# Two heads' v projections in one, and a mixed result written in place, in a hybrid decoder trunk

## The chip, the cores and the metric

The kernel runs on one core of a Trainium2 chip. The metric is the device time of one execution in microseconds (us). A core has TensorE (matrix products, into the accumulator memory PSUM), VectorE, ScalarE and GpSimd (element-wise work), and queues that issue transfers between the chip's main memory (DRAM here) and its on-chip memory (SBUF). The profile calls these engines PE (its weight loads PEld), DVE, ACT, POOL and SP.

## What is computed

Two layers over a residual stream of 1024 positions and 2048 channels, all in float32. Only layer 0 is touched by the change. Its mixer, cut to what matters:

```python
proj = h @ w_in                                   # 2048 -> 7 x 1024
a_u, a_v, a_z, q, k, v, b_z = split(proj)         # each 8 heads of 128 columns
# gating heads, in chunks of 128 positions
vh = rms_norm(gelu(a_v))                          # over each head
s = einsum('hts,bnshd->bnthd', tril(w_s), vh) + b_s
out_a = gelu(a_u) * s * silu(a_z)
# attention heads: stick-breaking, strictly causal, in blocks of 128 queries
z = q @ k.T / sqrt(128)
w = exp(log_sigmoid(z) + later)                   # later: sums of log_sigmoid(-z) to the right
out_b = (w @ v) * silu(b_z)
y = concat(out_a, out_b) @ w_out
```

Ahead of it, a modulation (silu(c) @ w_mod) gives shift, scale and gate of each layer. Layer 1 is a state-space layer whose matrices are prepared from small parameters.

## The kernel before

**Products.** Float32 weights are split exactly into two parts (`split`, L180 on ScalarE and L181 on VectorE), and each product is three matmuls (`mm3`, L205 to L208). `gemm` (L210) loads weights in raw chunks of 128 x 1024 elements, splits them in pieces of 512, and keeps four accumulators, one in each of the four PSUM banks of `ps_mm`; k is the outer loop, so all four banks are in use from the first to the last piece. At the end the banks are emptied one by one by `evac`; the next `gemm` gets its banks in turn. The buffers of a piece (`whi`, `wlo`) and of a raw chunk are three each.

**Layer 0, head by head.** The loop at L623 goes over eight pairs of a gating head and an attention head. In the order of the program, head h has: for even h above 0, the attention's gate projection of two heads (`bz`, L283 evacuates it); `proj_v` (L490), the gating's and the attention's v of one head; `gate_a(h-1)` (L595), the silu and gelu of the gates of the head before and its output product `sgu_out`, then the gelu of this head's `av`; `sgu_scale` and `sgu_mix` (the norm, then the mixing product `sg_ps` at L528, whose result is written to the tile `sg` at L529); the projection `qk`; `attention(h)`, whose first matmul is `z` (L552) and whose last is `oT` (L580); for heads 0 to 2 the modulation chunks (4, 6, 6 of them; `mod_chunk`, L466), for heads 3 to 7 steps of the state-space preparation (3, 4, 4, 4, 1; `s5_prep`); and the projection `uz`. For heads 2 and 4 `proj_v` stands ahead of `bz`. The table-switching functions of ScalarE are kept in runs (silu, gelu, exp and log) by `TableOrder`.

In `proj_v` the transposed input is the stationary operand (128 positions) and the weights are the moving one: 256 columns, 128 of the gating's v and 128 of the attention's. Positions are done in two halves of four banks. The other projections move 512 columns.

**What sets the order.** The program's order gives priorities. A planner puts the instructions of each engine in a fixed order by these priorities and its own costs, when the kernel is built, and inserts the waits. Tiles are taken from pools: a tag has so many buffers, given out in program order, and a new tile waits for the last reader of the old one. What matters here: `av` has one buffer and `v` two (each for one head); `sg` one; `q`, `k`, `u`, `zg` and the two `bz` one each; `ps_t`, a PSUM pool used by the attention, the column sums of the modulation chunks, the preparation and the mixing weight's transpose, has one; `ps_z` has two.

A modulation chunk streams 16 tiles `mraw` of 128 x 512 through four buffers, adds them up in `macc` on VectorE (L174) and sums over partitions on TensorE into `ps_t` (L158).

Of the kernel before, what the change touches and what calls it, by code (L numbers as in the profile page):

```python
# [18 lines left out]
L = 1024  # L19
# [6 lines left out]
class TableOrder:  # L26
    """Keeps the ScalarE functions that need different tables in separate runs."""
# [36 lines left out]
def hybrid_trunk(ctx: ExitStack, tc: tile.TileContext, x, c, ln_pre_g, ln_post_g, w_mod, b_mod,  # L64
# [75 lines left out]
    def rstd_from(ss, n, cnt, pool, name):  # L140
        """1/sqrt(ss/cnt + eps) of a [128, n] tile: exp(-log/2), then one Newton step."""
        r = pool.tile([128, n], F32, tag=name, name=name)
        v = pool.tile([128, n], F32, tag=name + "v", name=name + "v")
        t = pool.tile([128, n], F32, tag=name + "t", name=name + "t")
        V.tensor_scalar(out=v, in0=ss, scalar1=1.0 / cnt, scalar2=EPS, op0=ALU.mult, op1=ALU.add)
        tab.act(r, v, AF.Ln)
        tab.act(r, r, AF.Exp, scale=-0.5)
        V.tensor_tensor(out=t, in0=r, in1=r, op=ALU.mult)
        V.tensor_tensor(out=t, in0=t, in1=v, op=ALU.mult)
        V.tensor_scalar(out=t, in0=t, scalar1=-0.5, scalar2=1.5, op0=ALU.mult, op1=ALU.add)  # L150
        V.tensor_tensor(out=r, in0=r, in1=t, op=ALU.mult)
        return r

    def col_sums(ps, acc, n):
        """[128, n*128] partial sums -> [128, n] PSUM columns."""
        for i in range(n):
          with hi_prio():
            T.matmul(ps[:, i:i + 1], acc[:, i * 128:(i + 1) * 128], ones, start=True, stop=True)  # L158
# [24 lines left out]
    def load_raw(parts, ncols, dma=dma):  # L183
        """parts: (k, first column, DRAM slice [128, k, n]) -> raw tile [128, RAW]."""
        raw = wp.tile([128, RAW], F32, tag="wraw", name="wraw")
        rv = raw.rearrange("p (k n) -> p k n", n=ncols)
        for k, c0, src in parts:
            dma(out=rv[:, k:k + src.shape[1], c0:c0 + src.shape[2]], in_=src)
        return raw
# [3 lines left out]
    def load_w(parts, ncols, eng=V, raw=None, dma_=dma):  # L193
        """Yields the weight chunk in parts of SUB elements, split."""
        if raw is None:
            with hi_prio():
                raw = load_raw(parts, ncols, dma_)
        for i in range(RAW // SUB):
            with hi_prio():
                h = wp.tile([128, SUB], F32R, tag="whi", name="whi")  # L200
                lo = wp.tile([128, SUB], F32R, tag="wlo", name="wlo")
                split(h, lo, raw[:, i * SUB:(i + 1) * SUB], eng)
            yield h.rearrange("p (k n) -> p k n", n=ncols), lo.rearrange("p (k n) -> p k n", n=ncols)
# [6 lines left out]
    def gemm(nk, ncols, src, banks, evac, name, pre=None, eng=V):  # L210
        """src(k0, k1): parts of the weight rows; banks: (width, f), f(k, w_hi, w_lo) -> operands.

        k outermost, so that every weight chunk is used once; in the last chunk bank by bank."""
        ps = [mm_tile(name) for _ in banks]
        kr, ks = RAW // ncols, SUB // ncols
        k0 = 0
        for ci in range(nk // kr):
            if pre is not None:
                pre(ci)
            for wh, wl in load_w(src(ci * kr, (ci + 1) * kr), ncols, eng):  # L220
                if k0 + ks < nk:
                    for kk in range(ks):
                        for b, (wd, f) in enumerate(banks):
                            mm3(ps[b][:, :wd], *f(k0 + kk, wh[:, kk], wl[:, kk]), k0 + kk == 0, False)
                else:
                    for b, (wd, f) in enumerate(banks):
                        for kk in range(ks):
                            mm3(ps[b][:, :wd], *f(k0 + kk, wh[:, kk], wl[:, kk]), k0 + kk == 0, kk == ks - 1)
                        with hi_prio():
                            evac(b, ps[b])  # L230
                k0 += ks

# [19 lines left out]
    def banks_N(hf):  # L252
        res = []
        for t in range(4):
# [3 lines left out]
            res.append((256, f))  # L258
        return res

# [1 line left out]
    # h^T starts without the shift: its part of the first projections is a bias, and the shift is added to h^T later.  # L262
# [159 lines left out]
    with pool("pa") as pa, pool("pu") as pu_, pool("pst") as pst, pool("pat", 2) as pat, ExitStack() as pm_stack:  # L422
# [15 lines left out]
        def bias_first():  # L438
            """The shift's part of the first projections."""
            for gi, (s0, s1) in enumerate(first):  # L440
                ac = pm.tile([128, 512], F32, tag="macc", name="bacc")[:, 0:256]
                for ci in range(4):
                    if ci < 2:
                        ms = [pm.tile([128, 512], F32, tag="mraw", name="mraw", bufs=4) for _ in range(2)]
                    elif ci == 2:
                        ms = [pa.tile([128, L], F32, tag="sg", name="bw")]
# [19 lines left out]
        def mod_chunk(layer, n0):  # L466
            """512 columns of silu(c) @ w_mod, as partial sums over partitions."""
# [22 lines left out]
        def proj_v(h):  # L490
            av = pa.tile([128, 8, 128], F32, tag="av", name="av")
            v = pa.tile([128, 8, 128], F32, tag="v", name="v", bufs=2)
            st["av"], st["v"] = av, v
            for hf in range(2):
                def evac(b, ps, hf=hf):
                    S.activation(av[:, hf * 4 + b, :], ps[:, 0:128], AF.Copy)
                    st["v_done"] = S.activation(v[:, hf * 4 + b, :], ps[:, 128:256], AF.Copy).ins
                gemm(KT, 256, src_ab(1, 5, h), banks_N(hf), evac, f"v{h}e")

        def sgu_scale(h):  # L500
            """Per-token norm of gelu(v) over the head, in the exp/log run."""
            av = st["av"]
# [7 lines left out]
        def sgu_mix(h):  # L510
            av = st["av"]
# [11 lines left out]
            s = pa.tile([128, L], F32, tag="sg", name="sg")  # L523
# [16 lines left out]
        def attention(h):  # L540
            q, kT, v, bz = st["q"], st["k"], st["v"], st["bz"][h % 2]
# [53 lines left out]
        def gate_a(h):  # L595
            """Gates of gating head h, with gelu of the next head's v."""
# [12 lines left out]
            if h < 7:  # L609
                tab.act(st["av"], st["av"], AF.Gelu_apprx_tanh)  # L610
# [12 lines left out]
        for h in range(8):  # L623
            if h in (2, 4):
                proj_v(h)
            if h > 0 and h % 2 == 0:
                new_bz()
                proj_T(h, 6, None, evac_bz, "bz")
            if h not in (2, 4):
                proj_v(h)  # L630
            gate_a(h - 1)
# [38 lines left out]
    def pairs(ap, k0, cols):  # L670
        """Rows KORD[k0], KORD[k0 + 1] of ap [128, k, n], in one part if adjacent."""
# [314 lines left out]
def s5_prep(nc, tc, tab, const, pst, ps_t, ps_o, ident, dma, lam_re, lam_im, b_re, b_im, c_re, c_im,  # L986
            d_skip, log_dt, wb_d, wc_d, kk_d, et_d):
    """Matrices of the state space for chunks of 8 steps; a generator, two pairs of groups per step.

    Rows (g2 p): the 64 states of the two groups of a pair."""  # L990
# [310 lines left out]
```

## Time and profile before

| what | us |
|---|---|
| three runs | 2739.55, 2752.0, 2755.88 |
| median of them | 2752.0 |
| span of the profiled execution (its own time is not listed apart) | 2749.7 |
| PE busy in the span | 2603.6 (95%) |
| PEld | 2184.9 (79%) |
| DVE | 1771.3 (64%) |
| ACT | 1029.1 (37%) |
| POOL | 491.7 (18%) |

The span goes from the first to the last instruction. Times of day in the text are us from its start. The head loop of layer 0 takes roughly the stretch from 229 to 1670 us. A matmul's listed duration includes its way through the array, so matmuls in a row overlap; what one costs is the distance from start to start. A row of instructions gives the shortest, median and longest duration in ns, then the first and the last start.

### The profile page before, as it was taken

Reading aid. Unit: us, or ns where it says so; the run is one execution under the profiler, and the core shown is the slowest. Engines: PE = TensorE matmul, PEld = TensorE weight load, DVE = VectorE, ACT = ScalarE, POOL = GpSimd, SP = SyncE. Lnnn points to the kernel's source line nnn. Section 1 sums busy time; section 2 is a strip of 40 time slices with the busy share of each in tenths; the row PEclk is TensorE's granted clock in tenths of the full one; section 3 lists DMA queues with packets and bytes.
Section 4 is the critical chain, followed back from the end, with each engine's and each line's share of the span. In section 5 each row is a group of like instructions: output and inputs, shape, how many; then the busy total and the mean of one; then the engine's idle time right before and its main releaser. Section 6 shows DMA issues by size and latency. Waiting matters only on the chain.

```text
span 2749.7 us, 38891 instructions
## 1 busy us (share of the span) xinstructions
PE 2603.6 (95%) x13639; PEld 2184.9 (79%) x13639; DVE 1771.3 (64%) x4182; ACT 1029.1 (37%) x2035; POOL 491.7 (18%) x771
## 2 busy tenths in 40 slices
PE   4878999999999999999999999998999999999998
PEld 3657988988989878778888887787877888887876
DVE  7798877666766688888745464456364678546354
ACT  3444543333414314324434353444353222134332
POOL 2475000000001152340622400012030000002000
PEclk9989999999999999999999999999999999999999
DMA  8764656474571143332412235444254676454355
GB/s 287 270 208 124 203 164 198 146 238 147 184 238 56 58 111 83 100 95 62 141 54 90 86 100 181 153 156 135 93 183 150 207 222 191 132 186 158 126 194 170
DMA packets 356162, 417.97 MB, mean 152 GB/s; under 512 B 23632, under 2 KB 237952, under 8 KB 354560
## 3 DMA queue, kind: packets, MB, share of 16 engines
q1 hardware_dynamic: 346416, 392.95, 45.2%
q0 software_dynamic: 9552, 22.56, 2.5%
q8 instruction: 107, 1.75, 0.3%
q14 instruction: 87, 0.71, 0.1%
HBM read 355.62 MB, written 59.79 MB: 151 GB/s over the span
## 4 chain that ended last, share of the span: by engine, by line
PE 56%; DVE 20%; DMA 10%; issue 8%; ACT 4%; POOL 1%; SPq 1%; DVEq 0%; ACTq 0%; POOLq 0%
DVE wlo L181 2%; DMA mraw<-in_w_mod_dram 2%; DVE s5tc L1001 2%; DVE acc L174 2%; PE o0e L206 2%; PE o0e L208 2%; PE o0e L207 2%; PE o1e L206 2%; PE o1e L208 2%; PE o1e L207 2%; PE z L552 2%; PE oT L580 1%; DMA et_d<-s5et 1%; DVE y L732 1%; DMA wraw<-cat_d 1%
## 5 line engine op out<-in xcount | busy, mean ns | idle before, releaser
L180 ACT ACTIVATE whi<-wraw 128x512 fp32r<-128x512 f32 x632 | 395.1, 628 | 973.7 <-PE o1e L208 89.6
L181 DVE TENSOR_TENSOR wlo<-wraw,whi 128x512 fp32r<-128x512 f32 x592 | 423.4, 718 | 487.9 <-ACT whi L180 480.9
L174 DVE SCALAR_TENSOR_TENSOR macc<-mraw,cond,macc 128x512 f32<-128x512 f32 x240 | 180.1, 750 | 65.1 <-DMA mraw<-in_w_mod_dram 60.7
L207 PE MATMUL o1e<-wlo,catH 128*128 128x512 f32 x256 | 101.1, 395 | 3.9 <-DVE wlo L181 3.9
L207 PE MATMUL o0e<-wlo,catH 128*128 128x512 f32 x256 | 100.9, 394 | 0.0
L208 PE MATMUL o1e<-whi,catL 128*128 128x512 f32 x256 | 100.8, 394 | 0.0
L56 ACT ACTIVATE sp<-sp 128x128 f32<-128x128 f32 (+3 forms) x192 | 99.3, 521 | 3.7
L208 PE MATMUL o0e<-whi,catL 128*128 128x512 f32 x256 | 100.2, 393 | 0.0
L206 PE MATMUL o0e<-whi,catH 128*128 128x512 f32 x256 | 90.4, 396 | 6.8 <-ACT whi L180 3.9
L904 POOL TENSOR_TENSOR gt<-gt,zt 128x1024 f32<-128x1024 f32 x8 | 19.7, 2464 | 430.2 <-DMA gt<-g_d 430.2
L206 PE MATMUL o1e<-whi,catH 128*128 128x512 f32 x256 | 87.6, 393 | 2.2 <-ACT jk L704 2.0
L56 ACT ACTIVATE wt<-wt 128x128 f32<-128x128 f32 (+3 forms) x96 | 50.2, 523 | 104.8 <-DVE wt L569 93.0
L580 PE MATMUL oT<-wT,v 128*128 128x128 f32 x576 | 82.5, 280 | 5.9 <-DVE wT L578 5.9
L580 PEld LDWEIGHTS oT<-wT,v 128*128 128x128 f32 x576 | 76.4, 195 | 9.7 <-DVE wT L578 6.9
L735 POOL DMA_DIRECT2D x_d<-y x32 | 18.1, 566 | 368.7 <-DVE y L732 367.8
L56 ACT ACTIVATE sp<-z 128x128 f32<-128x128 f32 (+3 forms) x96 | 46.6, 487 | 88.2 <-PE z L552 87.1
L552 PE MATMUL z<-k,q 128*128 128x128 f32 (+3 forms) x192 | 78.2, 491 | 1.3 <-DVE wt L569 1.0
L174 DVE SCALAR_TENSOR_TENSOR acc<-m,cond,acc 128x512 f32<-128x512 f32 x60 | 72.8, 1213 | 8.0 <-DMA m<-in_w_mod_dram 6.7
L559 POOL TENSOR_SCALAR_AFFINE_SELECT sp<-sp 128x128 f32<-128x128 f32 x64 | 25.0, 390 | 279.8 <-DVE sp L557 216.2
L181 POOL TENSOR_TENSOR wlo<-wraw,whi 128x512 fp32r<-128x512 f32 x40 | 60.9, 1536 | 61.0 <-ACT whi L180 59.7
L1218 ACT ACTIVATE s5wb<-wb_ps 128x128 f32<-128x128 f32 x64 | 17.8, 277 | 140.7 <-DVE s5wb L1217 122.0
L578 DVE COPY wT<-wT_ps 128x128 f32<-128x128 f32 (+3 forms) x96 | 53.0, 553 | 21.0 <-PE wT_ps L576 20.6
(627 smaller groups left out, 8206.5 us busy)
## 6 DMA issues: line engine op xcount, KB each, us to landing
wraw<-in_w_in_ab_dram SPq DMA_DIRECT2D x268, 256.0 KB, 3.3
mraw<-in_w_mod_dram SPq DMA_DIRECT2D x256, 256.0 KB, 3.4
wraw<-in_w_in_ssm_dram SPq DMA_DIRECT2D x56, 512.0 KB, 4.5
wraw<-in_w_out_ab_dram SPq DMA_DIRECT2D x48, 512.0 KB, 3.8
raw<-in_w_mod_dram SPq DMA_DIRECT2D x16, 1024.0 KB, 6.6
m<-in_w_mod_dram SPq DMA_DIRECT2D x32, 512.0 KB, 4.5
wraw<-in_w_out_ssm_dram SPq DMA_DIRECT2D x32, 512.0 KB, 3.8
wraw<-in_w_in_ab_dram SPq DMA_DIRECT2D x17, 512.0 KB, 4.9
```

Source lines behind the costliest of these rows:

```text
L56: r = self.nc.scalar.activation(out, in_, func, **kw)
L174: V.scalar_tensor_tensor(out=acc, in0=m, scalar=cond[:, k:k + 1], in1=acc, op0=ALU.mult, op1=ALU.add)
L180: S.activation(h, r, AF.Copy)
L181: eng.tensor_tensor(out=lo, in0=r, in1=h, op=ALU.subtract)
L206: T.matmul(ps, sh, mh, start=first, stop=False)
L207: T.matmul(ps, sh, ml, start=False, stop=False)
L208: T.matmul(ps, sl, mh, start=False, stop=last)
L552: T.matmul(z[:, :w], q[:, i * 128:(i + 1) * 128], kT[:, k0:k1], start=True, stop=True)
L578: V.tensor_copy(wT[:, :w], pt[:, :w])
L580: T.matmul(oT, v[:, k0 // 128 + j, :], wT[:, j * 128:(j + 1) * 128], start=nb_done == 0, stop=nb_done == i)
L732: V.scalar_tensor_tensor(out=y[:, qs], in0=y[:, qs], scalar=r, in1=xr, op0=ALU.mult, op1=ALU.add)
L1001: V.tensor_tensor(out=o, in0=a, in1=b, op=ALU.mult)
```

## The change

`proj_v` is called for even heads only and projects the v of two heads: the moving operand has 512 columns, 256 of the gating's v and 256 of the attention's. The tiles `av` and `v` hold two heads, with one buffer each; the functions behind take the half of their head. `proj_v` comes after `gate_a(h-1)`, and `bz` always ahead of both; for head 0 `proj_v` comes first. The gelu of `av` is a function of its own, for both heads. `sgu_mix` writes its result over the `av` of its head, and the tile `sg` is gone; `bias_first`, which borrowed it, borrows two tiles of half the size. Besides, comments are taken out.

```diff
@@ banks_N
-            res.append((256, f))
+            res.append((512, f))
@@ bias_first
-                        ms = [pa.tile([128, L], F32, tag="sg", name="bw")]
+                        ms = [pat.tile([128, 512], F32, tag="wT", name="bw") for _ in range(2)]
@@ proj_v
-            av = pa.tile([128, 8, 128], F32, tag="av", name="av")
-            v = pa.tile([128, 8, 128], F32, tag="v", name="v", bufs=2)
+            av = pa.tile([128, 2, 8, 128], F32, tag="av", name="av")
+            v = pa.tile([128, 2, 8, 128], F32, tag="v", name="v")
             st["av"], st["v"] = av, v
+
+            def src(k0, k1):
+                return [(0, i * 256, w7[:, k0:k1, sl, h * 128:(h + 2) * 128]) for i, sl in enumerate((1, 5))]
+
             for hf in range(2):
                 def evac(b, ps, hf=hf):
-                    S.activation(av[:, hf * 4 + b, :], ps[:, 0:128], AF.Copy)
-                    st["v_done"] = S.activation(v[:, hf * 4 + b, :], ps[:, 128:256], AF.Copy).ins
-                gemm(KT, 256, src_ab(1, 5, h), banks_N(hf), evac, f"v{h}e")
+                    pv = ps.rearrange("p (a h d) -> p a h d", a=2, h=2)
+                    S.activation(av[:, :, hf * 4 + b, :], pv[:, 0], AF.Copy)
+                    st["v_done"] = S.activation(v[:, :, hf * 4 + b, :], pv[:, 1], AF.Copy).ins
+                gemm(KT, 512, src, banks_N(hf), evac, f"v{h}e")
@@ sgu_scale, sgu_mix
-            av = st["av"]
+            av = st["av"][:, h % 2]
@@ sgu_mix
-            s = pa.tile([128, L], F32, tag="sg", name="sg")
+            s = av.rearrange("p a b -> p (a b)")
@@ attention
-            q, kT, v, bz = st["q"], st["k"], st["v"], st["bz"][h % 2]
+            q, kT, v, bz = st["q"], st["k"], st["v"][:, h % 2], st["bz"][h % 2]
@@ gate_a
-            if h < 7:
-                tab.act(st["av"], st["av"], AF.Gelu_apprx_tanh)
+
+        def gelu_v():
+            for i in range(2):
+                tab.act(st["av"][:, i], st["av"][:, i], AF.Gelu_apprx_tanh)
@@ loop over the heads
-            if h in (2, 4):
+            if h == 0:
                 proj_v(h)
-            if h > 0 and h % 2 == 0:
+            elif h % 2 == 0:
                 new_bz()
                 proj_T(h, 6, None, evac_bz, "bz")
-            if h not in (2, 4):
-                proj_v(h)
             gate_a(h - 1)
+            if h > 0 and h % 2 == 0:
+                proj_v(h)
+            if h % 2 == 0:
+                gelu_v()
             tab.begin("explog")
```

## Rows read from the trace of the kernel before

**Rows 1.** Busy us (count) of PE, PEld, DVE, ACT, POOL by stretch; PE clock, DMA share, GB/s.

```profile
145.00:229.00 84.00, 64.56 (x267) 50.32 (x268) 77.27 (x68) 38.31 (x64) 63.62 (x38) 0.84 0.52 160
229.00:287.00 58.00, 52.14 (x404) 50.84 (x403) 44.97 (x73) 25.26 (x53) 19.93 (x14) 0.97 0.60 171
840.00:905.00 65.00, 65.00 (x514) 61.50 (x513) 43.55 (x77) 33.76 (x79) 6.12 (x16) 1.00 0.22 66
```

**Rows 2.** Chain that ended last, heads 1 to 2: start us, us, what.

```profile
515.44 0.89 PE oT L580 x8
520.01 0.80 PE cs L158 x8
...
522.20 4.94 DMA mraw<-in_w_mod_dram
...
563.61 1.04 PE cs L158 x8
...
640.94 1.78 PE sg_ps L528 x16
```

**Rows 3.** First matmuls `z` of each attention, heads 0 to 7, from line L552.

```profile
L552 PE MATMUL z<-k,q x24: 272/539/594, 311.5 to 360.5; 128*128 128x512 f32 x12, 128*128 128x128 f32 x4, 128*128 128x256 f32 x4, 128*128 128x384 f32 x4
...
L552 PE MATMUL z<-k,q x24: 270/539/595, 457.2 to 504.4; 128*128 128x512 f32 x12, 128*128 128x128 f32 x4, 128*128 128x256 f32 x4, 128*128 128x384 f32 x4
...
L552 PE MATMUL z<-k,q x24: 270/539/595, 647.1 to 699.1; 128*128 128x512 f32 x12, 128*128 128x128 f32 x4, 128*128 128x256 f32 x4, 128*128 128x384 f32 x4
...
L552 PE MATMUL z<-k,q x24: 270/539/595, 839.4 to 884.4; 128*128 128x512 f32 x12, 128*128 128x128 f32 x4, 128*128 128x256 f32 x4, 128*128 128x384 f32 x4
...
L552 PE MATMUL z<-k,q x24: 275/552/697, 1047.6 to 1100.0; 128*128 128x512 f32 x12, 128*128 128x128 f32 x4, 128*128 128x256 f32 x4, 128*128 128x384 f32 x4
...
L552 PE MATMUL z<-k,q x24: 270/540/697, 1220.9 to 1279.2; 128*128 128x512 f32 x12, 128*128 128x128 f32 x4, 128*128 128x256 f32 x4, 128*128 128x384 f32 x4
...
L552 PE MATMUL z<-k,q x24: 270/539/595, 1413.0 to 1468.8; 128*128 128x512 f32 x12, 128*128 128x128 f32 x4, 128*128 128x256 f32 x4, 128*128 128x384 f32 x4
...
L552 PE MATMUL z<-k,q x24: 270/539/697, 1578.9 to 1637.8; 128*128 128x512 f32 x12, 128*128 128x128 f32 x4, 128*128 128x256 f32 x4, 128*128 128x384 f32 x4
```

**Rows 4.** Column sums of five modulation chunks (eight each), and all mixing products.

```profile
L158 PE MATMUL gate_ps<-ones,macc x40: 165/250/271, 739.5 to 823.7; 128*128 128x1 f32 x40
...
L528 PE MATMUL sg_ps<-swt,av x128: 270/275/377, 307.1 to 1563.6; 128*128 128x128 f32 x128
```

**Rows 5.** PE in order of time around 905 us: start us, us, engine, line, instruction.

```profile
904.80 0.28 PE L206 MATMUL v4e<-whi,hTh 128*128 128x256 f32 x1
...
905.16 0.40 PE L206 MATMUL bz4e<-hTh,whi 128*128 128x512 f32 x1
905.40 0.40 PE L207 MATMUL bz4e<-hTl,whi 128*128 128x512 f32 x1
...
907.91 0.39 PE L206 MATMUL bz4e<-hTh,whi 128*128 128x512 f32 x1
```

**Rows 6.** Tiles v0e (its evacuation), bz4e and qk6e.

```profile
L496 ACT ACTIVATE av<-v0e x8: 257/278/333, 255.7 to 284.8; 128x128 f32<-128x128 f32 x8
...
L206 PE MATMUL bz4e<-hTh,whi x64: 388/389/502, 905.2 to 950.0; 128*128 128x512 f32 x64
...
L208 PE MATMUL qk6e<-hTh,wlo x64: 389/389/504, 1362.2 to 1409.2; 128*128 128x512 f32 x64
```

**Rows 7.** Last products of attentions 1 and 5, and ACT emptying bz6's last banks.

```profile
L580 PE MATMUL oT<-wT,v x72: 272/275/356, 471.0 to 521.5; 128*128 128x128 f32 x72
...
L580 PE MATMUL oT<-wT,v x72: 270/275/377, 1234.5 to 1303.8; 128*128 128x128 f32 x72
...
1309.13 1.96 ACT L283 ACTIVATE bz<-bz6e 128x512 f32<-128x512 f32 x2 [1.38 <-DMA cat_d<-bz]
```

**Rows 8.** The VectorE part of the weight split; busy us, mean ns, idle before it.

```profile
L181 DVE TENSOR_TENSOR wlo<-wraw,whi 128x512 fp32r<-128x512 f32 x592 | 423.4, 718 | 487.9 <-ACT whi L180 480.9 <-DMA wraw<-in_w_in_ab_dram 2.6 <-PE uz7e L208 2.0
```

**Rows 9.** Output projection: the last operand's split, and the first results read.

```profile
1676.06 0.63 ACT L180 ACTIVATE catH<-wraw 128x512 fp32r<-128x512 f32 x1 [3.18 <-DMA wraw<-cat_d]
...
L702 DVE TENSOR_TENSOR y<-o0e,gg x16: 681/683/692, 1690.1 to 1827.7; 128x512 f32<-128x512 f32 x16
```

More of the change, by code (lines that the diff above doesn't have):

```diff
@@ L510, in sgu_mix @@
         def sgu_mix(h):
-            av = st["av"]
+            av = st["av"][:, h % 2]
             with hi_prio():
@@ L623, in hybrid_trunk @@
         for h in range(8):
-            if h in (2, 4):
+            if h == 0:
                 proj_v(h)
-            if h > 0 and h % 2 == 0:
+            elif h % 2 == 0:
                 new_bz()
                 proj_T(h, 6, None, evac_bz, "bz")
-            if h not in (2, 4):
+            gate_a(h - 1)
+            if h > 0 and h % 2 == 0:
                 proj_v(h)
-            gate_a(h - 1)
+            if h % 2 == 0:
+                gelu_v()
             tab.begin("explog")
```

## The prediction

> **What bounds the kernel now.** I read three views, in this order. First the busy time by stretch [rows 1]: in layer 0 TensorE looks like the bound, for example 65.0 busy of 65.0 us between 840 and 905 us. The reader should not stop there, because this says only that something always stood ready to fill TensorE. So next the chain that ended last [rows 2]. In layer 0 it does not run along the projections: it goes from the last attention product of a head to the column sum of a modulation chunk, through the landings of `mraw`, to the next column sum, and at last to the gating's mixing product `sg_ps`, right before the next head's attention. Third, where each attention stands, by its first and last `z` matmul, eight rows for eight heads [rows 3]: 311.5 to 360.5, 457.2 to 504.4, 647.1 to 699.1, 839.4 to 884.4, and so on.
>
> The chain follows from one PSUM buffer. `ps_t` has a single slot, handed out in program order: attention h, then the modulation chunks (from head 3 on the steps of `s5_prep`), then the transpose of `sgu_mix(h+1)`, then attention h+1. The chunks come one at a time: the column sums of five of them start between 739.5 and 823.0 (the last matmul starts at 823.7), so 20.9 us each [rows 4]. From the last `z` of a head to the first of the next it thus takes 96.7, 142.7, 140.3, 163.2, 120.9, 133.8 and 110.1 us [rows 3]. There are two bounds, then, in balance: this chain, and TensorE, which does projections beside it.
>
> **What the change takes from TensorE.** Three 256-column matmuls take 904.80 to 905.16, so 0.120 us from start to start; 512-column ones take 0.228 (eleven steps from 905.40 to 907.91) [rows 5], and 192 of these fill 905.2 to about 950.6 [rows 6], 45.4 us, as the changes of banks at the end add 1.6. The eight projections are 8 x 384 = 3072 matmuls of 256 columns, after the change 1536 of 512. Saved: 1536 x (2 x 0.120 - 0.228) = 18 us. By columns alone at 2.4 GHz the two would be 0.107 and 0.213, so 13 to 15 ns of each matmul is fixed, and half of these fixed parts go. The Trainium skill (TensorE: Matmul & The Clock Gate, Back-to-back issue gap) gives columns over 2.4 GHz plus 2.5 ns for an isolated matmul; by that the saving would be 1536 x 2.5 ns = 4 us. The trace's fixed part is five times as long, and the trace decides.
>
> **What hardly counts.** The weights are loaded in as many transfers of the same 256 KB (16 chunks a pair, two transfers each), and split in as many pieces: one piece served 24 matmuls x 0.120 = 2.9 us, now 12 x 0.228 = 2.7 us. The evacuations become half as many of twice the width; they took 0.278 us each [rows 6], 35 us of ScalarE for 128 of them, so the gain there lies between 0 and 17 us, off the path (I take 0). The gelu covers the same elements, two at once per pair. Writing the mixed result over `av` adds no instruction; `bias_first` loads two half tiles for one. SP's and POOL's queues carry what they did.
>
> **What is moved, and the waits it adds.** `v` has one buffer for a pair where it had two for single heads, and `av` is now held until `sgu_out` of the pair's second head. Three things follow.
>
> 1. The second head's share of the pair comes before attention 0. The first projection ended at 284.8 + 0.3 [rows 6]; the pair needs 2 x 192 x 0.228 = 87.6 us for 384 x 0.120 = 46.1, that is 41 us more, and 1 us for the second gelu. Attention 0 starts at 311.5 + 42 = 353.5.
>
> 2. Ahead of an even head the pair's projection can't be evacuated before the odd head's attention has read `v` and `sgu_out` has read `av`. Worse, the bz projection now always stands before it, and its second pair of banks is held until the odd attention's result has been stored. Head 6 shows that already: its last attention product starts at 1303.8, the bz banks are emptied from 1309.1 on, after the DMA [rows 7]. All four `ps_mm` banks are thus taken or blocked while the odd attention runs. Before, for heads 2 and 4, the next v projection ran there. Next to run on TensorE are therefore, in a row after an odd attention: 3 us until banks come free (5 to 7, less some matmuls in the two free banks), two halves of 45.4, the qk projection 45.4, and 3 us for evacuation and first `z` (qk6 ended near 1409.6, `z` came at 1413.0 [rows 3, 6]): 142 us from the end of an odd attention to the next even one, where the chain alone needed 125.6 (521.5 to 647.1 [rows 3, 7]).
>
> 3. In the odd attention TensorE has only what is left of uz and bz, and its own work: 65 - 46.1 = 19 us [rows 1]. It idles there, and with fewer splits beside it the attention gets shorter. A split costs VectorE 0.718 us [rows 8], every 2.9 us beside a v projection, 25% of VectorE. From first to last `z` the shortest so far took 45.0 us [rows 3]; without splits it lies between 45 x 0.75 = 34 and 45. I take 40 for heads 1 and 3. Even ones, now beside uz and qk with splits half as often, took 49 to 56; I take 46, 48, 50, 51 (low end 4 us less, high end their old lengths). Heads 5 and 7 (58 and 59) have `s5_prep` beside them: 50 and 55 (44 to 58, 50 to 59).
>
> **The sum**, first `z` by first `z`, with the gaps of before where the chain rules and 17 us from last `z` to the end of an attention (504.4 to 521.5):
> - head 0 at 353.5, last `z` 399.5; head 1 at +96.7 = 496 (457.2 before)
> - last `z` 536, end 553; head 2 at +142 = 695 (647.1)
> - last `z` 743; head 3 at +140.3 = 883 (839.4)
> - 923, end 940; head 4 at the later of 923 + 163.2 and 940 + 150 (142 and 8 of preparation on TensorE) = 1090 (1047.6)
> - 1140; head 5 at +120.9 = 1261 (1220.9)
> - 1311, end 1328; head 6 at +150 = 1478 (1413.0)
> - 1529; head 7 at +99 = 1628 (1578.9), as the last `sg_ps` at 1563.6 [rows 4] allowed 11 us less than the 110.1, which qk7 had set
> - last `z` at 1683, 45 us after the 1637.8 of before.
>
> The output projection can't take its last operand before that. There were 11 us of slack: the last `catH` split began at 1676.1, some 3 us suffice from there, and the first result was read at 1690.1 [rows 9]. So 45 - 11 = 34 us later, and nothing behind it changes. The 18 us saved on TensorE are in the 41 and the 142 already, and lie beside waits elsewhere. The profiled span of 2749.7 becomes 2783.7. The profile gives no other time for that execution; the median of the three runs, 2752.0, is 2.3 us over the span, so I add 2.3: **2786 us**.
>
> **Ends.** Attentions at the low ends take 40 us off in sum, at the high ends add 36: 2746 and 2822. TensorE sets the floor: no more than its 18 us can go, 2734.
>
> **Rivals.**
> - *The attentions shrink enough* (not slower). If each gets 4.3 us shorter than I took it, the 34 us are gone; from there on it is no slower. For it: VectorE lost a quarter of its load there. Against it: an attention is a chain through four engines with two buffers. Time at the low ends: 2746.
> - *TensorE is the only bound* and every gap gets filled: 2752 - 18 = 2734. For it: 65.0 busy of 65.0 us, and much the same in most of layer 0. Against it: the chain of [rows 2] touches few projections. A planner's new order could even go below by a little.
> - *The uncovered attentions slow down too.* The granted clock falls where TensorE has gaps: 0.84 in a stretch with 64.6 us busy of 84.0, against 1.00 when full [rows 1]. At the lower of the two levels, 1.2 GHz, the 19 us of an attention's own work become 38; if half of that is on its path, heads 1, 3 and 5 end about 10 us later each: 2816. The Trainium skill (TensorE: Matmul & The Clock Gate, What's actually happening) says that throttling is the default and activity lifts it; the stretch agrees.
> - *No gain from the wider matmul.* The 18 us vanish; they stand in the sum four times, before heads 0, 2, 4 and 6: 2804, within my range.
>
> **How the numbers follow.** A measurement can tell about 1%, 27 us, from no change. The forecast, with its neighbourhood of 2768 to 2805, has 0.38 (0.08 of it within 1%); shrinking attentions 0.28, all within 1%; TensorE alone 0.14, half of it below 2724 through a better order; slower attentions 0.16, and no gain or an order that is worse still 0.04, both slower. Faster 0.07, to which I add 0.03 for what I can't see in a replanned order (taken from within 1%): 0.10. Same: 0.08 + 0.28 + 0.07 - 0.03 = 0.40. Slower: 0.30 + 0.16 + 0.04 = 0.50. The range runs from 2738, near the floor, to 2824, past the high ends.
>
> **What would show it.** The changed profile should have 1536 matmuls of 128x512 with an interval of 0.228 us in the v projections; attention 0 starting at about 353; column sums still 20 us apart; TensorE idle by 20 to 30 us inside the attentions of heads 1 and 3, with a lower granted clock; the first evacuation of v2 a few us after attention 1 ended; the last `z` of head 7 near 1683. The prediction is wrong if TensorE stays full through the odd attentions, if attention 1 starts before 475, or if the last `z` comes by 1650.

## The result and the profile after

The changed kernel takes **2853.2 us** (median of four runs, 2844.8 to 2857.5), the kernel before, beside it, 2745.8 (2738.9 to 2755.9): a ratio of **1.037**, with a 95% interval from 1.035 to 1.040. It is slower by 107 us. The forecast was 2786, slower by 34, with a range up to 2824: the sign was right, the size a third of the true one.

The page of the changed kernel begins with its span; then the busy time of each engine, and the granted clock of TensorE in 40 slices:

```profile
span 2855.8 us, 35803 instructions
...
PE 2633.7 (92%) x12103; PEld 2122.5 (74%) x12103; DVE 1764.5 (62%) x4182; ACT 1027.0 (36%) x1971; POOL 487.6 (17%) x771
...
PEclk9889999899999899999999998899999999999999
```

The span grew by 106.1. Where, show the rows that answer to [rows 3]: the `z` matmuls of heads 0 to 7.

```profile
L558 PE MATMUL z<-k,q x24: 270/540/595, 356.1 to 411.7; 128*128 128x512 f32 x12, 128*128 128x128 f32 x4, 128*128 128x256 f32 x4, 128*128 128x384 f32 x4
...
L558 PE MATMUL z<-k,q x24: 270/634/1222, 511.1 to 553.8; 128*128 128x512 f32 x12, 128*128 128x128 f32 x4, 128*128 128x256 f32 x4, 128*128 128x384 f32 x4
...
L558 PE MATMUL z<-k,q x24: 270/539/595, 716.9 to 773.4; 128*128 128x512 f32 x12, 128*128 128x128 f32 x4, 128*128 128x256 f32 x4, 128*128 128x384 f32 x4
...
L558 PE MATMUL z<-k,q x24: 270/592/1222, 915.6 to 953.4; 128*128 128x512 f32 x12, 128*128 128x128 f32 x4, 128*128 128x256 f32 x4, 128*128 128x384 f32 x4
...
L558 PE MATMUL z<-k,q x24: 270/539/595, 1128.8 to 1185.7; 128*128 128x512 f32 x12, 128*128 128x128 f32 x4, 128*128 128x256 f32 x4, 128*128 128x384 f32 x4
...
L558 PE MATMUL z<-k,q x24: 270/592/697, 1314.6 to 1370.9; 128*128 128x512 f32 x12, 128*128 128x128 f32 x4, 128*128 128x256 f32 x4, 128*128 128x384 f32 x4
...
L558 PE MATMUL z<-k,q x24: 270/539/595, 1530.7 to 1587.2; 128*128 128x512 f32 x12, 128*128 128x128 f32 x4, 128*128 128x256 f32 x4, 128*128 128x384 f32 x4
...
L558 PE MATMUL z<-k,q x24: 272/540/697, 1701.1 to 1752.0; 128*128 128x512 f32 x12, 128*128 128x128 f32 x4, 128*128 128x256 f32 x4, 128*128 128x384 f32 x4
```

The last `z` comes 114.2 us later than before (1752.0 for 1637.8). The output projection gives 11 of them back: its last operand's split began 14.0 us before the first result was read [rows 9], and now does so 8.9 us before; and from the last `z` to that split it took 38.3 us, now 32.2.

```profile
1784.17 0.63 ACT L180 ACTIVATE catH<-wraw 128x512 fp32r<-128x512 f32 x1 [1.06 <-DMA wraw<-cat_d]
...
L712 DVE TENSOR_TENSOR y<-o0e,gg x16: 679/681/692, 1793.1 to 1934.6; 128x512 f32<-128x512 f32 x16
```

So the first result is read 103.0 us later (1793.1 for 1690.1), and what comes behind takes 3 us more, 1062.7 for 1059.6. Nearly all of the loss lies in the head loop.

Inside it the heads part by their parity. From the rows above, an attention takes from its first to its last `z` 55.6, 42.7, 56.5, 37.8, 56.9, 56.3, 56.5, 50.9 us; before, 49.0, 47.2, 52.0, 45.0, 52.4, 58.3, 55.8, 58.9 [rows 3]. The odd ones got shorter, by 2 to 8 us; the even ones longer, by 0.7 to 6.6. Heads 0 to 3 again in the view of busy time by stretch, from the first `z` to the last product `oT` (columns as in [rows 1]):

```profile
356.00:435.00 79.00, 79.00 (x396) 64.68 (x396) 46.60 (x81) 38.65 (x72) 4.97 (x16) 1.00 0.14 41
511.00:567.00 56.00, 37.87 (x154) 25.49 (x152) 36.73 (x67) 26.89 (x51) 4.62 (x16) 0.80 0.08 25
717.00:800.00 83.00, 83.00 (x415) 68.26 (x414) 46.08 (x82) 38.56 (x71) 6.13 (x16) 1.00 0.15 45
916.00:966.00 50.00, 33.64 (x147) 23.05 (x145) 33.20 (x62) 23.05 (x48) 4.90 (x16) 0.85 0.00 0
```

In the even ones TensorE never rests, in the odd ones it rests for a third of the time, at a clock of 0.80 and 0.85. The whole loop in one line each, from the start of the first projection to the first result read, the kernel before and then the changed one:

```profile
229.40:1690.00 1460.60, 1424.04 (x8162) 1216.75 (x8162) 1018.17 (x2958) 560.98 (x1187) 300.06 (x608) 0.99 0.43 131
```

```profile
230.50:1793.00 1562.50, 1451.05 (x6631) 1152.08 (x6629) 1018.98 (x2959) 558.59 (x1124) 298.01 (x608) 0.97 0.40 122
```

Idle time of TensorE there: 36.6 us before, 111.5 after. There are 1531 fewer matmuls (1536 by the count; a few records are missing), and yet 27 us more busy time; that fits the lower clock (0.97 for 0.99), and that a matmul which stands alone is listed with its full way through the array, 0.39 us for an interval of 0.228. How the 27 us divide between the two was not measured.

Of the 111.5 us, 56 lie in the four odd attentions, from the first `z` to the last product (5 before), and 39 between the end of one attention and the next (19 before). The even attentions are not idle; while they last, and behind them, TensorE does projections that have to be done anyway. But it gets so far ahead that the odd attention finds none left: the last matmul of `bz2e` starts at 509.5, 1.6 us before the first `z` of attention 1.

```profile
L208 PE MATMUL bz2e<-hTh,wlo x64: 389/389/476, 462.9 to 509.5; 128*128 128x512 f32 x64
```

### The profile page after: what moved, and what is told of

It reads as the page before. It is cut to its first block, busy times and chain, and to the rows that moved or that the text cites. A ratio compares the mean times of both kernels' runs of the same rounds, so it can differ in the third digit from the quotient of the medians.

```text
span 2855.8 us, 35803 instructions
## 1 busy us (share of the span) xinstructions
PE 2633.7 (92%) x12103; PEld 2122.5 (74%) x12103; DVE 1764.5 (62%) x4182; ACT 1027.0 (36%) x1971; POOL 487.6 (17%) x771
## 4 chain that ended last, share of the span: by engine, by line
PE 33%; DVE 8%; issue 6%; DMA 5%; ACT 2%; POOL 1%; SPq 0%; DVEq 0%; POOLq 0%; ACTq 0%
PE o1e L206 2%; PE o1e L207 2%; PE o1e L208 2%; PE o0e L206 1%; PE o0e L207 1%; PE o0e L208 1%; DVE wlo L181 1%; DMA wraw<-cat_d 1%; DMA xr<-in_x_dram 1%; PE su1e L206 1%; PE su1e L208 1%; PE su1e L207 1%; DVE y L742 1%; DVE wt L569 1%; DVE s5tc L1011 1%
## 5 line engine op out<-in xcount | busy, mean ns | idle before, releaser
L586 PEld LDWEIGHTS oT<-wT,v 128*128 128x128 f32 x576 | 83.4, 207 | 56.2 <-DVE wT L584 48.2
L586 PE MATMUL oT<-wT,v 128*128 128x128 f32 x576 | 90.7, 298 | 36.7 <-DVE wT L584 35.0
L558 PE MATMUL z<-k,q 128*128 128x128 f32 (+3 forms) x192 | 86.8, 538 | 17.3 <-DVE wt L575 13.6
L56 ACT ACTIVATE sp<-z 128x128 f32<-128x128 f32 (+3 forms) x96 | 46.8, 488 | 115.5 <-PE z L558 113.9
L563 DVE SCALAR_TENSOR_TENSOR sp<-z,sp 128x128 f32<-128x128 f32 (+3 forms) x96 | 52.8, 550 | 43.2 <-ACT sp L56 42.9
L584 DVE COPY wT<-wT_ps 128x128 f32<-128x128 f32 (+3 forms) x96 | 53.0, 552 | 34.3 <-PE wT_ps L582 34.0
```

The lines of the kernel that those rows point to most:

```text
L56: r = self.nc.scalar.activation(out, in_, func, **kw)
L558: T.matmul(z[:, :w], q[:, i * 128:(i + 1) * 128], kT[:, k0:k1], start=True, stop=True)
L563: V.scalar_tensor_tensor(out=a[:, :w], in0=z[:, :w], scalar=0.0, in1=a[:, :w], op0=ALU.max, op1=ALU.add)
L584: V.tensor_copy(wT[:, :w], pt[:, :w])
L586: T.matmul(oT, v[:, k0 // 128 + j, :], wT[:, j * 128:(j + 1) * 128], start=nb_done == 0, stop=nb_done == i)
```

## The experiments

The kernel before ran beside each group of runs, at 2750.8 (runs 1 to 4), 2755.4 (5 to 8) and 2751.0 us (9 to 12). Ratios are to it. The changed kernel was timed only beside the 2745.8 above; so a distance from it carries 5 to 10 us of doubt, and where it matters the distance by the ratios stands beside it.

**1. Pairing without the wider matmul.** The order, the buffers and the waits of the change, but each head's v with 256 columns.

```diff
-            res.append((512, f))
+            res.append((256, f))
...
-            for hf in range(2):
-                def evac(b, ps, hf=hf):
...
-                gemm(KT, 512, src, banks_N(hf), evac, f"v{h}e")
+            for i in range(2):
+                for hf in range(2):
+                    def evac(b, ps, hf=hf, i=i):
...
+                    gemm(KT, 256, src_ab(1, 5, h + i), banks_N(hf), evac, f"v{h}e")
```

> The changed kernel with its order and buffers kept, but the pair's v projection again as two projections of 256 moving columns (12 x 2 us of ns-sized steps more on TensorE). Theory C (the loss comes from what covers the attentions: one v buffer for a pair, bz ahead of it): the loss stays and the narrower matmuls add their 18 us or less: 2850 to 2880 us, attention 2 still 50 to 60 us from first to last z. Rival W (512 moving columns with the weights as moving operand are what slows it): back to 2740 to 2780. Rival P (writing the mixed result in place, which holds av until sgu_out): no change, 2845 to 2860, not told apart from C by this run.

Measured 2877.2 us (1.047, 1.044 to 1.050), 24 us slower than the changed kernel (26 by the ratios). So the width saves time, and what loses lies in the order and the buffers. Not all of the 24 us need be the matmuls': this run also has twice as many evacuations of half the width. The attentions are of the same two kinds: 56.8, 37.8, 56.5, 36.7 us for heads 0 to 3.

**2, 3, 4. One part of the change alone, on the kernel before.** One buffer for `v`; the `bz` projection always ahead of the v projection; the mixed result over `av` (with two `av`, as there the next head's v may come early).

```diff
-            v = pa.tile([128, 8, 128], F32, tag="v", name="v", bufs=2)
+            v = pa.tile([128, 8, 128], F32, tag="v", name="v")
```

> The kernel before with one buffer for v instead of two, nothing else. Theory C: no v projection can be evacuated beside an attention any more, so TensorE runs short inside the attentions and every head's gap grows: 2790 to 2860. Rivals W and P: v's buffers don't matter, 2735 to 2765.

```diff
-            if h in (2, 4):
-                proj_v(h)
...
-            if h not in (2, 4):
-                proj_v(h)
+            proj_v(h)
```

> The kernel before with bz ahead of the v projection for heads 2 and 4 too, as it has it for head 6. Theory C: attentions 1 and 3 lose the v projection as cover and have bz, whose second pair of banks stays blocked; 10 to 30 us for the two of them, 2755 to 2780. Rivals W and P: 2735 to 2765.

```diff
-            av = pa.tile([128, 8, 128], F32, tag="av", name="av")
+            av = pa.tile([128, 8, 128], F32, tag="av", name="av", bufs=2)
...
-            s = pa.tile([128, L], F32, tag="sg", name="sg")
+            s = av.rearrange("p a b -> p (a b)")
```

> The kernel before with only the in-place write: the mixed result goes over its own av, which gets two buffers of one head each (the same memory as av and sg together before); the bias's borrowed tile becomes two halves as in the change. Theory C: 2735 to 2760, no difference. Rival P: 2790 or more.

Measured: 2772.9 (1.009, 1.006 to 1.012), 2775.3 (1.010, 1.007 to 1.013) and 2753.7 (1.001, 1.000 to 1.003). One buffer costs 22 us, less than the 40 that I had expected at least; the order of `bz` costs 24, as expected; writing in place costs nothing that can be told from noise. Run 3, the order of `bz`, held a hint that I had not looked for. With `bz`, at 512 columns, beside attentions 1 and 3 in the place of v, at 256, these two took 57.8 and 56.3 us, for 47.2 and 45.0 before:

```profile
L552 PE MATMUL z<-k,q x24: 270/540/595, 454.7 to 512.5; 128*128 128x512 f32 x12, 128*128 128x128 f32 x4, 128*128 128x256 f32 x4, 128*128 128x384 f32 x4
...
L552 PE MATMUL z<-k,q x24: 270/539/595, 850.1 to 906.4; 128*128 128x512 f32 x12, 128*128 128x128 f32 x4, 128*128 128x256 f32 x4, 128*128 128x384 f32 x4
```

From this came theory F: the fixed order lays a number of projection matmuls between the steps of an attention, its cover. Where TensorE is full, the attention lasts as long as they do, plus its own work; and the pairing replaced 256-column ones beside the even attentions by 512-column ones.

**5. The changed kernel with narrow cover.** `uz` of even heads and `qk` of odd heads, which stand beside the even attentions, with two matmuls of 256 columns for each of 512 (but for the first and the last product of a bank). The projections as a whole are the same, in smaller grains; how many grains lie beside an attention is the planner's choice, made anew for each kernel.

```diff
-        T.matmul(ps, sh, ml, start=False, stop=False)
...
+        cols = st.get("cols", (slice(None),))
...
+        for c in cols:
+            T.matmul(ps[:, c], sh, ml[:, c], start=False, stop=False)
...
+                if h % 2:
+                    st["cols"] = (slice(0, 256), slice(256, 512))
                 proj_T(h, 3, 4, evac_qk, "qk")
+                st.pop("cols", None)
...
+                if h % 2 == 0:
+                    st["cols"] = (slice(0, 256), slice(256, 512))
                 proj_T(h, 0, 2, evac_uz, "uz", ((0,), (1,)) if h == 7 else ((0, 1),))
+                st.pop("cols", None)
```

> The changed kernel, with the projections that stand beside the even attentions (uz of even heads, qk of odd heads) issued as two matmuls of 256 columns in place of one of 512, bar the first and the last product of a bank. Theory F (the planner lays a fixed count of projection matmuls between the steps of an attention, by its own costs; 176 of 512 columns take TensorE longer than 254 to 284 of 256): from first to last z the even attentions fall from 56 us to 45 to 50, with shorter tails, and the total to 2790 to 2830 although TensorE has up to 10 us more to do. Rival A (an even attention is held by ScalarE and VectorE, or by the kind of projection beside it): still 56 us, total 2850 to 2870.

Measured 2813.5 (1.021, 1.018 to 1.024): **40 us faster than the changed kernel** (46 by the ratios), though TensorE has more to do. Head 2's attention:

```profile
L562 PE MATMUL z<-k,q x24: 271/539/594, 704.3 to 746.7; 128*128 128x512 f32 x12, 128*128 128x128 f32 x4, 128*128 128x256 f32 x4, 128*128 128x384 f32 x4
```

It takes 42.4 us where the changed kernel took 56.5. The even attentions are 42.1, 42.4, 50.3 and 42.4. What lay beside them is seen by asking for one tile in the stretch of an attention (length, then busy time and count of PE, its weight loads and ACT for that tile, then clock, DMA share and GB/s). First `uz2e` in the changed kernel and in this one, then `v4e` and `v1e` beside attentions 3 and 0 of the kernel before, then `v2e` beside attention 1 of the changed one:

```profile
716.90:773.40 56.50, 45.42 (x177) 32.92 (x176) 2.36 (x4) 1.00 0.13 38
```

```profile
704.30:746.70 42.40, 34.13 (x232) 29.41 (x231) 0.00 (x0) 1.00 0.09 27
```

```profile
839.40:884.40 45.00, 36.20 (x254) 31.96 (x255) 1.81 (x8) 1.00 0.20 59
...
311.50:360.50 49.00, 40.78 (x286) 35.81 (x284) 1.88 (x8) 1.00 0.50 152
```

```profile
511.10:553.80 42.70, 3.75 (x13) 2.10 (x12) 0.00 (x0) 0.80 0.09 30
```

With the intervals of [rows 5], 177 x 0.228 = 40.4 us of cover go with 56.5 us; 286 x 0.120 = 34.3 with 49.0; 254 x 0.120 = 30.5 with 45.0; 232 x 0.120 = 27.8 with 42.4. The cover plus some 15 us gives each of them (in the first, seven matmuls of `qk3e` come to the 177). On a TensorE that is full such a sum has to come out; what the run adds is that the attention got shorter when less was laid beside it, 232 matmuls of 256 columns in the place of 177 of 512. With almost nothing beside it, 13 and 16 matmuls, attentions 1 and 3 of the changed kernel still take 43 and 38 us, with TensorE idle in them: something else of their chain rules there.

What was not done beside the even attentions is left for the odd ones: 89 matmuls of `bz2e` lie beside attention 1 and 116 of `bz4e` beside attention 3, where the changed kernel has none of either. These two took 46.3 and 48.6 us, longer than in the changed kernel, and yet the loop from the first projection to the first result read got shorter by 44 us, as TensorE's idle time in it fell from 111.5 to 80.5:

```profile
231.10:1749.90 1518.80, 1438.33 (x7919) 1208.28 (x7918) 1018.34 (x2960) 557.44 (x1124) 294.66 (x608) 0.98 0.41 126
```

**6. The changed kernel with other modulation counts.** One chunk less behind attention 0 and one more behind attention 1; two preparation steps moved from behind attention 4 to behind attention 5.

```diff
-        NMOD = (4, 6, 6)
-        NPREP = (0, 0, 0, 3, 4, 4, 4, 1)
+        NMOD = (3, 7, 6)
+        NPREP = (0, 0, 0, 3, 2, 6, 4, 1)
```

> The changed kernel with the background work redistributed: modulation chunks 3, 7, 6 instead of 4, 6, 6 behind heads 0, 1, 2, preparation steps 3, 2, 6, 4, 1 instead of 3, 4, 4, 4, 1 behind heads 3 to 7. Theory C (between an even and an odd attention the chain of chunks or steps rules and TensorE runs dry, between an odd and an even one TensorE rules): attention 1 starts 20 us earlier (490), attention 5 some 60 us earlier in all, the total falls to 2785 to 2820. Rival B (TensorE's work or the projection order rules everywhere): 2845 to 2860.

Measured 2823.0 (1.025, 1.023 to 1.027), 30 us faster than the changed kernel (34 by the ratios), 3 us short of the range that I expected. Behind an even attention the chain of chunks or steps rules, behind an odd one TensorE does; moving work of the chain from the first kind of gap to the second one starts attention 1 at 489.9 instead of 511.1 and attention 5 at 1243.5 instead of 1314.6. From the last `z` of attention 0 to the next head's first it takes 79.5 us for 99.4, with a chunk less; from that of attention 1, with a chunk more, 162.8 for 163.1. Behind attention 5 the rule holds less well: with two steps more it takes 190.6 for 159.8, and of the 71 us won at attention 5 there are 36 left at attention 6 (1494.7 for 1530.7).

**7. Both of these together.**

> The two changes before together. Theories C and F: the gains add up as long as TensorE does not run full, 2745 to 2790. If only one of them holds, the time of that one.

Measured 2797.8 (1.016, 1.014 to 1.018): 55 of the 70 us that the two give alone, and 8 us above the range that I expected. From the end of attention 5 to the start of attention 6 it now took 178 us, 148 in the changed kernel.

**8. The cover left out.** The changed kernel without `uz` of head 2 and without `qk` of head 3.

```diff
-            if h > 0:
+            if h > 0 and h != 3:
...
-            else:
+            elif h != 2:
                 new_uz()
```

> The changed kernel without the uz projection of head 2 and the qk projection of head 3 (left out; the tiles keep what they held). Theory F: attention 2 has nothing beside it and falls from 56.5 us (first to last z) to 36 to 43, as attentions 1 and 3 have it, its tail from 27 to 12, and the whole by the 30 us of these or a little more, not by the 90 us of TensorE work left out. Rival A: attention 2 stays at 50 us or more.

Measured 2827.0 (1.027, 1.023 to 1.030). Inconclusive for what it was made for. The planner put the next projection, `uz` of head 3, in the freed place, 177 matmuls of 512 columns again, and attention 2 took 54.9 us, for 56.5; attention 3, which now had nothing beside it, took 39.5. That fits F, but the run does not show attention 2 uncovered.

**9 and 10. The same two cures on the kernel before.** First one step moved from behind attention 4 to behind attention 5; then, with it, `uz` of head 5 and `bz` of head 6 in narrow grains beside attention 5.

```diff
-        NPREP = (0, 0, 0, 3, 4, 4, 4, 1)
+        NPREP = (0, 0, 0, 3, 3, 5, 4, 1)
```

> The kernel before with one preparation step moved from behind head 4 to behind head 5 (3, 3, 5, 4, 1). Theory C: attention 5 was held by the steps (99 us behind attention 4) and starts some 20 us earlier, attention 6 is held by TensorE and doesn't mind; TensorE has 7 us idle between 1131 and 1300 to win back: 3 to 10 us faster than before, 2740 to 2750 beside 2752. If TensorE's work rules all of it: no change.

> The same, and the projections beside attention 5 (uz of head 5, bz of head 6) in matmuls of 256 columns. Theory F: attention 5 falls from 58 us (first to last z) to 45 to 50, its tail from 25 to 18; as TensorE rules from there on, the total gains 0 to 8 us more, less the 5 us that the narrow matmuls cost. Rival: attention 5 keeps 58 us.

Measured 2750.8 (1.000, 0.998 to 1.002) and 2751.6 (1.001, 0.999 to 1.002); the 3 to 10 us that I expected of the first did not come. In it, attention 5 starts 25 us earlier (1195.8 for 1220.9), and attention 6 at 1413.8, where it was (1413.0). In the second, attention 5 takes 46 us instead of 58, again as F says, and nothing comes of it. In the kernel before, TensorE is busy 1424 of 1461 us of the loop, and a shorter chain buys nothing. What cured part of the changed kernel's loss cures nothing here, where there is hardly any idle time to win back.

**11 and 12. How far the cure goes.** Run 7 with one of the steps moved back; then, with it, all `uz`, `bz` and `qk` of heads 1 to 7 narrow.

> As the run with both changes, but preparation steps 3, 3, 5, 4, 1 instead of 3, 2, 6, 4, 1. There attention 6 started 178 us behind attention 5, where 148 had been enough before. If the six steps beside the pair's projection made that, it falls to 150 to 165 and the total to 2780 to 2795; if not, 2795 to 2815.

> The same, with all uz, bz and qk projections of heads 1 to 7 in matmuls of 256 columns; only the pair's v keeps 512. Theory F: attentions 5 and 7 fall by 10 us each too; TensorE has about 2 us per projection more to do, which matters only where it rules: 2765 to 2795. If narrow matmuls help only even heads: 2790 to 2820.

Measured 2799.6 (1.018, 1.015 to 1.021) and 2792.8 (1.015, 1.012 to 1.019). The step that was moved back is not what kept run 7 above its expectation. The time of run 12 lies in both of the ranges that I had set for it and tells nothing between them; its attentions do. In it the odd attentions are covered too, all eight take 42 to 48 us, and TensorE is full in them; here the stretches of attentions 1 and 5 and the whole loop:

```profile
468.00:531.00 63.00, 63.00 (x490) 59.13 (x489) 43.03 (x78) 30.45 (x60) 5.99 (x17) 1.00 0.22 70
1214.00:1277.00 63.00, 63.00 (x490) 59.10 (x489) 59.59 (x274) 28.35 (x58) 5.62 (x18) 1.00 0.20 52
230.30:1721.70 1491.40, 1446.78 (x9754) 1300.85 (x9754) 1018.97 (x2958) 558.46 (x1123) 296.12 (x608) 0.99 0.42 129
```

The idle time is down to 44.6 us, near the 36.6 of before, but the busy time is 22.7 us above that of before at the same clock, for 1592 matmuls more: 14.3 ns each, the fixed part that the forecast had put at 13 to 15. So the narrow cover gives back what the wide v had saved: of the 31 us by which this loop is longer than before, 23 are such busy time and 8 idle time. No version beat the kernel before.

## Why the prediction was wrong in size

The forecast was a sum from first `z` to first `z`; so the miss can be laid out step by step, from the rows above.

| step | forecast us | measured us |
|---|---|---|
| first `z` of head 0 | 353.5 | 356.1 |
| head 0 to 1 | 142.5 | 155.0 |
| 1 to 2 | 199 | 205.8 |
| 2 to 3 | 188 | 198.7 |
| 3 to 4 | 207 | 213.2 |
| 4 to 5 | 171 | 185.8 |
| 5 to 6 | 217 | 216.1 |
| 6 to 7 | 150 | 170.4 |
| head 7, first to last `z` | 55 | 50.9 |

The end is 1683 by the one and 1752.0 by the other, 69 us apart. The four steps from an even head miss 12.5 + 10.7 + 14.8 + 20.4 = 58 of them, the three from an odd head 12, the start 3, and head 7 gives back 4.

**Right: head 0.** The second head's share of the pair before attention 0 was put at 42 us and took 44.6.

**Right in kind: the order of the even heads.** `bz` with its banks held until the odd attention is stored, then two halves of v and qk in a row. The banks of `bz2e` are emptied after the transfer, and the pair's v follows in 512-column matmuls of 0.225 us (four steps from 592.05 to 592.95):

```profile
572.39 1.96 ACT L283 ACTIVATE bz<-bz2e 128x512 f32<-128x512 f32 x2 [7.81 <-DMA cat_d<-bz]
...
592.05 0.39 PE L207 MATMUL v2e<-wlo,hTh 128*128 128x512 f32 x1
...
592.95 0.39 PE L208 MATMUL v2e<-whi,hTl 128*128 128x512 f32 x1
```

From the last product of attention 1 to the next `z` it took 150 us (566.5 to 716.9), for 142; from that of attention 3, 164 (965.1 to 1128.8), for 150. Shorter tails of these attentions (13 and 12 us from the last `z` to the end, for the 17 that I took) hid 10 of the 22 us. TensorE was idle for 10 and 14 us of these stretches, where I had allowed 6, and in the first 12 us behind attention 1 the granted clock stood at the lower level, 1.2 GHz:

```profile
566.50:578.50 12.00, 5.45 (x15) 4.09 (x14) 6.81 (x10) 5.36 (x5) 0.00 (x0) 0.50 0.81 264
```

One sign that I had named for this step failed: v2's first evacuation was to come a few us after attention 1 ended. It came at 617.4, because only 18 of its 384 matmuls had run by then, and nearly the whole first half was still to do.

**Right: the odd attentions.** Forecast 40, 40, 50, 55, measured 42.7, 37.8, 56.3, 50.9, with TensorE idle by 18 and 16 us and a lower clock in heads 1 and 3; for the idle time I had named 20 to 30 us. The rival that this clock slows them is right in kind and too large in size. They took less at 0.80 and 0.85 than at 1.00 before, but that comparison mixes the clock with the lost cover. One without that lies in run 6: there attention 3 has 16 matmuls of `v4e` beside it, as in the changed kernel, and takes 34.8 us at a clock of 0.95, for 37.8 at 0.86 (run 6, then the changed kernel):

```profile
894.60:929.40 34.80, 23.79 (x112) 15.93 (x110) 27.18 (x51) 19.96 (x43) 4.68 (x15) 0.95 0.00 0
```

```profile
915.60:953.40 37.80, 26.68 (x111) 17.74 (x110) 27.14 (x51) 19.96 (x43) 4.61 (x15) 0.86 0.00 0
```

So the price is nearer 3 us than the 10 of that rival, by one pair of attentions that was not made for it.

**Right: the chain of chunks.** Five column sums still start between 819.4 and 899.9, 20 us apart. The slack at the output projection was 11 us, as taken, but by luck: no run shows that some 3 us suffice behind the last operand's split; it was 8.9 us, and the rest of the 11 came from the 6 us by which that split followed sooner on the last `z`.

**Wrong: the even attentions, and with them the steps from even to odd heads.** The failed step is "Even ones, now beside uz and qk with splits half as often, took 49 to 56; I take 46, 48, 50, 51". I sized them by VectorE's load, since a matmul of twice the width needs half the splits in a given time. They took 55.6, 56.5, 56.9 and 56.5, above their old lengths, the high ends that I gave, in all four. Not VectorE sets their length but the time that the cover takes on a full TensorE: 177 matmuls of 512 columns, 40.4 us, where head 0, for one, had 286 of 256 columns, 34.3 us. That is 30.5 us of the 58. The rest is in the time from the last `z` to the next head's first, which I took over from before: it grew by 3, 2, 8 and 4 us, and for the last of them I had taken 11 off (see below). The tails in it, from the last `z` to the end of the attention, grew: from 19 to 23 us in head 0 (its last product, below, starts at 434.4, its last `z` at 411.7) and from 19 to 27 in head 2 (800.0 and 773.4). The last products have the cover between them too; in the odd heads 1 and 3, without it, the tails went down to 13 and 12. As head 2's tail grew by 8 us and its whole time between by 2, the tails do not explain that part head by head.

```profile
L586 PE MATMUL oT<-wT,v x72: 270/275/377, 369.8 to 434.4; 128*128 128x128 f32 x72
...
L586 PE MATMUL oT<-wT,v x72: 272/275/582, 518.2 to 566.5; 128*128 128x128 f32 x72
...
L586 PE MATMUL oT<-wT,v x72: 270/275/356, 730.3 to 800.0; 128*128 128x128 f32 x72
```

And from head 6 to 7 I had taken 11 us off for a product that seemed to come earlier; 113.9 us were measured there, more than the old 110.1. Run 5 shows the cause: with the same program order and buffers, but narrow cover in an order planned anew, the steps from the even heads take 139.7, 179.4, 165.4 and 140.2 us, below the forecast of each.

[Rows 3] could have told it. In the kernel before, head 6 has `uz` with 512 columns beside it and takes 55.8 us, while heads 3 and 0, with v at 256 columns, take 45.0 and 49.0. I had not compared them. The cover of head 6 needs fewer splits than theirs, VectorE has less to do beside it, and yet its attention is the longer one, which speaks against VectorE. In the kernel before, first `uz6e` beside attention 6, then the busy time of all engines in attentions 6 and 3 (31 us of VectorE in 55.8, and 33 in 45.0):

```profile
1413.00:1468.80 55.80, 45.48 (x177) 32.92 (x176) 2.36 (x4) 1.00 0.13 38
```

```profile
1413.00:1468.80 55.80, 55.80 (x275) 45.22 (x274) 30.87 (x57) 26.84 (x55) 5.88 (x15) 1.00 0.13 38
839.40:884.40 45.00, 45.00 (x345) 41.69 (x344) 33.37 (x61) 27.17 (x63) 5.82 (x15) 1.00 0.20 59
```

**Slightly short: the width.** Run 1 puts it at 24 us for 1536 matmuls saved, 15.6 ns each if all of it is theirs; I took 18, and the doubt of run 1's figure covers that. By the rule of the Trainium skill (TensorE: Matmul & The Clock Gate, Back-to-back issue gap), 2.5 ns for an isolated matmul, it would have been 4 us, an estimate from that figure. The runs disagree with it.

**The other rivals.** TensorE as the only bound would have given a faster kernel; its idle time tripled instead. The shrinking attentions came true for the odd heads alone. No gain from the width is refuted by run 1.

**What stays open.** The two parts of the order that could be tried alone cost 22 and 24 us, and the pairing as such, at 256 columns, 126. Both act on the same buffers and the same cover, so the numbers do not add up, and no run splits the 126 further. A pair with two buffers of `v`, ahead of `bz`, was not tried. Why the planner lays 177 wide matmuls beside an attention, or 232 to 286 narrow ones, no run shows; the runs show what the choice does to the time. And what rules an attention that has no cover was not looked into.

## What to carry to other kernels

When a chain of dependent steps, here an attention, runs on a full TensorE beside other matmuls in a fixed order, its length is the time of that cover plus its own work; changing the width of the cover, or which projection it is, changes the chain, even where the total work falls. And what the cover does early is missing later, where the engine then idles. So before a projection is merged or moved, list for each chained stage what lies beside it now and what will, in counts times the interval from the trace, and look for stages that end up with none. And a merge that must hold its buffer across two stages can pay for it twice, as here: at the first stage, which waits for the second one's share (attention 0 started 44.6 us later), and at the stage that loses its cover (TensorE idle by 18 and 16 us).

## What was not expected of the hardware

- A stage with the engine a third idle can be shorter than the same stage with it full: 37.8 us at a clock of 0.85, for 45.0 at 1.00 with the cover. In it single `z` matmuls took up to 1222 ns, for 595 at most in a covered one.
- The fixed part of a matmul came out alike in two ways: 13 to 15 ns from the intervals and 14.3 from the busy time of run 12. Run 1, by its total time, gives 15.6, with the doubt said there.
